# Ten products by ones into an unread bank, set among the first adaLN groups on TensorE, ahead of the first product of q

## The chip, the core and the metric

The kernel runs on one core of one Trainium2 chip. The metric is the device time of one execution in microseconds (us), the median of several runs of the same program. A core has TensorE (PE, which multiplies; PEld is its loading of weights), VectorE (DVE), ScalarE (ACT), GpSimd (POOL) and SyncE (SP, which here only issues transfers). Each works through its own instructions in order and waits on semaphores for the others. Products go to PSUM, which has eight banks of 128 partitions x 512 float32; everything else on the chip is in SBUF.

## What is computed

One step of a decoder trunk for 512 prompt positions and 8 sample positions, 1024 wide, all in float32. The part that the change touches is its beginning: the modulation of adaLN, the first RMSNorm, and the product that makes q (the other columns of `w_in`, attention, a recurrent branch and the feed-forward part follow).

```python
def rms_norm(x, g):
    xf = x.astype(jnp.float32)
    y = xf * lax.rsqrt(jnp.mean(xf * xf, axis=-1, keepdims=True) + EPS)
    return (y * g.astype(jnp.float32)).astype(x.dtype)

def ada_modulation(c, ada_w, ada_b):
    m = (jax.nn.silu(c) @ ada_w + ada_b)[:, None, :]
    return jnp.split(m, 6, axis=-1)
...
    sh1, sc1, g1, sh2, sc2, g2 = ada_modulation(c, ada_w, ada_b)
    h = rms_norm(x, norm1_g) * (1.0 + sc1) + sh1
    z = h @ w_in
```

The ten products that the change adds are no part of this: nothing reads them.

## The kernel before, in words

Everything is held transposed: features lie on the 128 partitions, the 520 positions along the row, so `x` is eight tiles `x[0]` to `x[7]` of 128 x 520. A product over all positions is made in two halves of 260 (`HALF`). To keep float32 accuracy, both factors of a large product are split into a rounded part and a rest (`whi`, `wlo` for weights, `hh`, `hl` for h), and three products of the faster type fp32r are summed: hi x hi, lo x hi, hi x lo. The small products at the beginning are made in float32 itself; for each of these the profile records two passes (two MATMUL records).

The beginning runs so:

- SP issues the loads in the order of the code: parameters (`prm`), constants (`cs`, which holds the identity and a square of ones, `ones`), the eight tiles of `x`, then eight tiles `araw` of 512 KB, the first half of adaLN's weights for shift and scale (line 473), then three loads of weights of q (`wraw`, line 510), then eight more `araw` tiles for the second half. The `araw` tiles share seven buffers, so the eighth waits until the first has been multiplied.
- ACT squares the tiles of `x`, DVE adds the squares up, and TensorE sums over partitions by multiplying with `ones` into the banks `ss1_0` and `ss1_1` (line 543: four products of 128 x 260).
- `first_mod(0, ...)` (lines 470 to 478): for each of the eight `araw` tiles (`kq` 0 to 7) four products, 32 columns wide, side by side in the array, accumulate into the bank `adaf0`. I call these four products a group. A group waits for its tile.
- `first_mod_end(0, ...)` (lines 480 to 494): ACT copies the bank (line 482), TensorE turns it by two transposes (line 485), and DVE makes the modulation from it (`mod`, line 489; `n1amp`, line 493).
- `first_h(f)` (lines 496 to 505): for each of the first four feature tiles ACT makes `hh` (line 499; the eight sample positions by a small copy, line 503), POOL the eight sample positions (lines 500, 501), DVE the exact value (line 502) and the rest `hl` (line 504). Between them ACT and DVE split the weights of q into `whi` (line 517) and `wlo` (line 518).
- `q_matmuls` (lines 522 to 528): the products of q over the first half of the features, into six banks at a time (`qp0_0`, `qp0_1` and so on). The eight groups of the second half of adaLN (`first_mod(1, ...)`, bank `adaf1`) are set among them, one after every nine products in the steady part.

TensorE takes all of this in one order, which the framework's scheduler fixes when the program is built. `tc.issue_after(m)` puts an instruction behind `m` in it. `bank(name)` takes one of the eight PSUM banks and gives it back after its last use.

Of the kernel before, what the change touches and what calls it, by code (L numbers as in the profile page):

```python
# [24 lines left out]
KT = 8  # L25
# [3 lines left out]
HALF = NT // 2  # L29
# [36 lines left out]
def kernel(ctx, tc, xT, par, gates, b_f, cst, cse, own, cache_k, cache_v, cache_lf, pt,  # L66
# [3 lines left out]
    pe, act, dve, pool, sp = nc.tensor, nc.scalar, nc.vector, nc.gpsimd, nc.sync  # L70
# [9 lines left out]
    def slot(name, cols=NT, dt=F32, parts=128):  # L80
        return heap.tile([parts, cols], dt, name=name, tag="slot")

    def bank(name, parts=128, cols=512):
        return psp.tile([parts, cols], F32, name=name, tag="bank")
# [9 lines left out]
    x = []  # L94
# [9 lines left out]
    ident = cs[:, C_ID:C_ID + 128]  # L104
    ones = cs[:, C_ONE:C_ONE + 128]
# [5 lines left out]
    silc = keep.tile([128, KT, 32], F32, name="silc")  # L111
# [47 lines left out]
    for jt in range(FF // 128):  # L159
# [5 lines left out]
        for name in BLOCKS:  # L165
            units.append((c, name, 4))
            if name in JOIN[jt]:
                g, i = JOIN[jt][name]
# [301 lines left out]
    def first_mod(fh, acc, kqs):  # L470
        for kq in kqs:
            raw = pgp.tile([128, 2, 512], F32, name="araw", tag="pg")
            sp.dma_start(raw, ada_w[kq * 128:kq * 128 + 128, :2048].rearrange("p (v c) -> p v c", v=2)
                         [:, :, 512 * fh:512 * fh + 512])
            for g in range(4):
                pe.matmul(acc[32 * g:32 * g + 32, :256], lhsT=silc[:, kq],
                          rhs=raw[:, g // 2, 256 * (g % 2):256 * (g % 2) + 256],
                          start=kq == 0, stop=kq == KT - 1, tile_position=(0, 32 * g))

    def first_mod_end(fh, acc):  # L480
        sb = slot("adas", 256)
        act.copy(sb, acc[:, :256])
        tp = bank(f"adaft{fh}")
        for b in range(2):
            pe.transpose(tp[:, b * 128:b * 128 + 128], sb[:, b * 128:b * 128 + 128], ident)
        tv = tp[:, :256].rearrange("p (b g c) -> p b g c", b=2, g=4)
        fs = slice(4 * fh, 4 * fh + 4)
        for v in (1, 0):
            dve.tensor_tensor(
                mod[:, v, fs].rearrange("p (q b) c -> p b q c", b=2), tv[:, :, 2 * v:2 * v + 2, 0:9],  # L490
                prm[:, fs, P_AB + v:P_AB + v + 1].rearrange("p (q b) c -> p b q c", b=2).to_broadcast([128, 2, 2, 9]),
                ALU.add)
        dve.scalar_tensor_tensor(amp1[:, fs], mod[:, 1, fs], 1.0, prm[:, fs, P_N1:P_N1 + 1].to_broadcast([128, 4, 9]),
                                 ALU.add, ALU.mult)
# [35 lines left out]
    def wraw():  # L530
        return wp.tile([128, KT, 256], F32, name="wraw", tag="wraw", bufs=2)

    ssq = [bank(f"ss1_{j}") for j in range(2)]
    for f in range(KT):
        t = slot("sq1")
# [5 lines left out]
        if f % 4 == 3:  # L541
            for j, (t0, t1) in enumerate(HALVES):
                pe.matmul(ssq[j][:, :HALF], lhsT=ones, rhs=sq[:, t0:t1], start=f == 3, stop=f == KT - 1)
    acc = [bank(f"adaf{fh}") for fh in range(2)]
    first_mod(0, acc[0], range(KT))
    r1 = slot("r1")
    for j, (t0, t1) in enumerate(HALVES):
# [6 lines left out]
    raw = wraw()  # L554
    q_weights(0, raw, 0, 0)
    first_mod_end(0, acc[0])
    for f in range(4):
        first_h(f)
    q_weights(0, raw, 4, 2)
    raw = wraw()  # L560
    q_weights(0, raw, 0, 4)
    for g3 in (0, 3):
        banks = [bank(f"qp{i}_{j}") for i in range(g3, g3 + 3) for j in range(2)]
        for k in range(4):
            for n in range(6):
                q_matmuls(0, g3 + n // 2, n % 2, k, banks[n])
                if g3 == 0 and n % 3 == 2:
                    first_mod(1, acc[1], (2 * k + n // 3,))
            if g3 and k == 0:
                first_mod_end(1, acc[1])  # L570
                for f in range(4, KT):
                    first_h(f)
        for n in range(6):
            t0, t1 = HALVES[n % 2]
            act.copy(qpart[g3 + n // 2][:, t0:t1], banks[n][:, :HALF])
        if g3 == 0:
            flr = slot("flr", KT * H).rearrange("p (k c) -> p k c", k=KT)
            sp.dma_start(flr, w_in[:, COL_FL:COL_FL + H].rearrange("(k p) c -> p k c", p=128))
    raw = wraw()
    q_weights(1, raw, 0, 0)  # L580
    q_weights(1, raw, 4, 2)
    raw = wraw()
# [312 lines left out]
    for i in range(KT):  # L895
        if i % 4 == 0:
            qtp.append(bank(f"qt{i}", NS))
        if i < 6:
            t = qpart[i]
            for j, (t0, t1) in enumerate(HALVES):  # L900
                b = bank(f"q{i}_{j}")
# [43 lines left out]
    g = [None] * KT  # L945
# [390 lines left out]
    g = None  # L1336
# [306 lines left out]
    for j in range(2):  # L1643
        for m in range(2 * PLAIN):
            if j == 0:
                begin(u + 3)
            b = bank(f"fi{m}_{j}")
# [89 lines left out]
```

## Time and profile before

| | |
|---|---|
| time, median of 3 runs | 1028.36 us (1027.15 to 1031.1) |
| the profiled execution | 1033.71 us, its span 1032.1 us |
| PE busy | 997.7 us (97%), 7994 records |
| DVE busy | 793.5 us (77%) |
| ACT busy | 552.5 us (54%) |
| POOL busy | 330.7 us (32%) |
| chain that ended last | PE 77%, DVE 10%, DMA 5%, ACT 4%, issue 3% |
| mean of the 16 DMA engines' traffic | 201 GB/s |

The page divides the span into 40 slices of 25.8 us; the first slice and the second hold everything that the change touches. Times inside the kernel are counted from the start of the span. A view by windows gives, for any stretch, how long each engine was busy in it, with the number of instructions in brackets, and then the clock that TensorE was granted (1.00 is full), the busy share of the DMA engines and what they moved. A timeline has one row for an instruction or a run of equal ones: start, duration, engine, line, operation, what is written and read, and, in square brackets, how long the engine had been idle and what ended that. [...] The chain of waits is the chain of work that ended last, with each piece cut at the point where the next takes over.

### The profile page before, as it was taken

To read this page: it belongs to the slowest core of one execution; us is meant where nothing else is said; L and a number is where in the kernel's file an instruction comes from. 1 tells how busy PE (TensorE), PEld (TensorE's weight loads), DVE (VectorE), ACT (ScalarE), POOL (GpSimd) and SP (SyncE) were. 2 spreads that over 40 slices of the span, in tenths; PEclk is the share of its full clock that TensorE was granted. 3 is DMA by queue.
4 is the path that set the end of the run, shared out by engine and by line. 5 is a ranking of instruction groups with operands and counts; after the bars stand their busy time and mean duration, and the time that the engine had idled before them with its cause. 6 is when DMAs were issued, how large, how long until landed. Compare 5 with 4: busy or idle time off the path is not lost.

```text
span 1032.1 us, 21298 instructions
## 1 busy us (share of the span) xinstructions
PE 997.7 (97%) x7994; PEld 922.1 (89%) x7994; DVE 793.5 (77%) x1423; ACT 552.5 (54%) x1132; POOL 330.7 (32%) x424
## 2 busy tenths in 40 slices
PE   4999999999999999999999999999999999999996
PEld 1888989999898988878888989999999999999996
DVE  5446999998999977886756544778878888888864
ACT  4433665857682266776876223555444444445453
POOL 0214511111135134554430001485433423424212
PEclk9899999999999999999999999999999999999998
DMA  9888987878898998999665784323343342333212
GB/s 330 298 270 290 306 288 210 274 230 274 260 272 297 340 322 254 295 283 275 197 240 183 251 304 139 83 62 100 86 123 88 98 124 65 99 104 102 62 63 83
DMA packets 164378, 206.98 MB, mean 201 GB/s; under 512 B 9890, under 2 KB 125106, under 8 KB 164210
## 3 DMA queue, kind: packets, MB, share of 16 engines
q1 hardware_dynamic: 147554, 152.52, 47.7%
q0 software_dynamic: 13040, 46.67, 13.8%
q10 hardware_dynamic: 3680, 6.42, 1.7%
q8 instruction: 63, 1.03, 0.4%
q14 instruction: 41, 0.34, 0.1%
HBM read 192.49 MB, written 13.09 MB: 199 GB/s over the span
## 4 chain that ended last, share of the span: by engine, by line
PE 77%; DVE 10%; DMA 5%; ACT 4%; issue 3%; POOL 1%; SPq 0%; POOLq 0%; DVEq 0%; ACTq 0%
PE fo L305 12%; PE pb L305 4%; PE gb L305 4%; PE k L305 4%; PE v L305 3%; PE ga L305 3%; PE pa L305 3%; PE wo L305 3%; PE pv L817 2%; PE gr L305 2%; PE xr L305 2%; DMA wraw<-in_w_in_dram 2%; PE qp L527 2%; PE po L1265 2%; PE q L527 1%
## 5 line engine op out<-in xcount | busy, mean ns | idle before, releaser
L246 ACT CAST whi<-wraw 128x1024 fp32r<-128x1024 f32 (+1 forms) x79 | 82.1, 1040 | 135.2 <-PE pb L305 35.3
L248 DVE TENSOR_TENSOR wlo<-wraw,whi 128x1024 fp32r<-128x1024 f32 (+1 forms) x79 | 100.1, 1268 | 31.3 <-ACT whi L246 29.2
L270 ACT CAST wb<-ws 128x512 fp32r<-128x512 f32 x72 | 44.8, 622 | 92.2 <-PE fo L305 64.4
L305 PE MATMUL fo<-ach,wb 128*128 128x260 f32 x512 | 93.2, 282 | 0.0
L682 POOL DMA_DIRECT2D pg<-in_cache_k_dram x74 | 39.4, 533 | 141.8 <-DVE S L731 76.1
L305 PEld LDWEIGHTS fo<-ach,wb 128*128 128x128 f32 x512 | 78.9, 188 | 0.0
L271 DVE TENSOR_TENSOR wb<-wraw,wb 128x512 fp32r<-128x512 f32 x86 | 74.0, 860 | 6.0 <-ACT wb L270 5.0
L261 POOL TENSOR_TENSOR ws<-wraw 128x512 f32<-128x512 f32 x18 | 26.7, 1485 | 153.7 <-DMA wraw<-in_w_fi_dram 135.1
L270 ACT CAST wb<-wraw 128x512 fp32r<-128x512 f32 x86 | 53.4, 621 | 37.1 <-ACT cp L1625 6.2
L305 PE MATMUL fo<-acl,wb 128*128 128x260 f32 x256 | 72.3, 282 | 0.0
L271 DVE TENSOR_TENSOR wb<-ws,wb 128x512 fp32r<-128x512 f32 x72 | 59.9, 832 | 15.1 <-ACT wb L270 13.3
L730 DVE TENSOR_TENSOR pg<-pg,qb 128x1024 f32<-128x1024 f32 x48 | 58.4, 1236 | 1.3 <-DMA pg<-in_cache_k_dram 1.2
L731 DVE TENSOR_REDUCE S<-pg 128x16 f32<-128x1024 f32 x48 | 57.1, 1210 | 0.1
L1222 POOL TENSOR_SCALAR p<-p,mu 128x128 f32<-128x128 f32 (+3 forms) x28 | 35.6, 1282 | 51.6 <-DVE mu L1218 39.6
L305 PEld LDWEIGHTS fo<-acl,wb 128*128 128x128 f32 x256 | 48.2, 188 | 0.0
L1216 ACT ACTIVATE p<-p,mu 128x128 f32<-128x128 f32 (+3 forms) x64 | 35.3, 553 | 13.6 <-DVE mu L1215 13.3
L305 PE MATMUL v<-hh,whi 128*128 128x260 f32 x128 | 37.9, 296 | 0.6 <-DVE pl L1236 0.3
L305 PE MATMUL pb<-oh,whi 128*128 128x260 f32 x128 | 36.9, 288 | 1.0 <-ACT oh L1323 1.0
L305 PE MATMUL k<-hh,whi 128*128 128x260 f32 x128 | 37.3, 292 | 0.0
L817 PE MATMUL pv<-pg,pw 128*32 128x512 f32 x256 | 35.1, 604 | 2.0 <-DMA pg<-in_cache_v_dram 1.8
L305 PE MATMUL ga<-hh,wlo 128*128 128x260 f32 x128 | 36.3, 284 | 0.8 <-DVE wlo L248 0.8
L305 PE MATMUL gb<-hh,whi 128*128 128x260 f32 x128 | 37.0, 289 | 0.0
(1099 smaller groups left out, 3980.6 us busy)
## 6 DMA issues: line engine op xcount, KB each, us to landing
araw<-in_ada_w_dram SPq DMA_DIRECT2D x48, 512.0 KB, 6.9
wraw<-in_w_fi_dram SPq DMA_DIRECT2D x44, 512.0 KB, 4.1
pg<-in_cache_k_dram POOLq DMA_DIRECT2D x42, 512.0 KB, 6.2
pg<-in_cache_v_dram SPq DMA_DIRECT2D x42, 512.0 KB, 5.2
wraw<-in_w_in_dram SPq DMA_DIRECT2D x34, 512.0 KB, 7.3
wraw<-in_w_in_dram SPq DMA_DIRECT2D x11, 1024.0 KB, 10.4
pg<-in_cache_v_dram POOLq DMA_DIRECT2D x22, 512.0 KB, 6.6
pg<-in_cache_k_dram POOLq DMA_DIRECT2D x32, 256.0 KB, 5.9
```

The source lines that it names most:

```text
L246: state["act"] = act.copy(hi[:, :k1 - k0], src)
L248: state["last"] = dve.tensor_tensor(lo[:, :k1 - k0], src, hi[:, :k1 - k0].bitcast(F32), ALU.subtract)
L270: state["act"] = act.copy(t[:, :4], src)
L271: state["last"] = dve.tensor_tensor(t[:, 4:], src, t[:, :4].bitcast(F32), ALU.subtract)
L305: state["mm"] = pe.matmul(out[:, :t1 - t0], lhsT=wt[k], rhs=at, start=k == 0 and m == 0, stop=k == nk - 1 and m == 2)
L527: state["mm"] = pe.matmul(b[:, :HALF], lhsT=wt, rhs=at[:, t0:t1], start=k == 0 and m == 0, stop=k == 3 and m == 2)
L682: done.append(eng.dma_start(pg, cache[bass.ds(r, 1), :, c0:c1].rearrange("a p c -> (a p) c")))
L730: dve.tensor_tensor(pg, pg, q, ALU.mult)
L731: last = dve.tensor_reduce(S[r // 2][:, c:c + H], pg.rearrange("p (h d) -> p h d", d=DH), AX.X, ALU.add)
L817: pe.matmul(pv[0][32 * gq:32 * gq + 32, :], lhsT=pw[r][:, c:c + 32], rhs=pgs[gq // 2][:, 512 * hf:512 * hf + 512], start=j == 0, stop=j == ...
L1216: act.activation(p[:, :n + 128], p[:, :n + 128], AF.Exp, bias=mu[:, 0:1], scale=-1.0, accum_out=mu[:, 1:2])
L1222: (pool.tensor_scalar(p, p, mu[:, 2:3], None, ALU.mult) if a and i + 1 < KT else act.activation(p, p, AF.Copy, scale=mu[:, 2:3]))
```

## The change

A ninth name for a bank, `idle`, is taken before the others. Behind each of the groups `kq` 2 to 7 of `first_mod(0, ...)`, TensorE multiplies the first 260 positions of `x[0]` by `ones` into it once, and behind the two transposes of `first_mod_end(0, ...)` four times: ten float32 products of 128 x 260. Nothing reads the bank. The second half of adaLN (`fh == 1`) gets none.

```diff
             for g in range(4):
-                pe.matmul(acc[32 * g:32 * g + 32, :256], lhsT=silc[:, kq],
-                          rhs=raw[:, g // 2, 256 * (g % 2):256 * (g % 2) + 256],
-                          start=kq == 0, stop=kq == KT - 1, tile_position=(0, 32 * g))
+                m = pe.matmul(acc[32 * g:32 * g + 32, :256], lhsT=silc[:, kq],
+                              rhs=raw[:, g // 2, 256 * (g % 2):256 * (g % 2) + 256],
+                              start=kq == 0, stop=kq == KT - 1, tile_position=(0, 32 * g))
+            if fh == 0:
+                keep_busy(m, 1 if kq > 1 else 0)
+
+    def keep_busy(m, n):
+        for _ in range(n):
+            with tc.issue_after(m.ins):
+                m = pe.matmul(idle[:, :HALF], lhsT=ones, rhs=x[0][:, :HALF], start=True, stop=True)
 
     def first_mod_end(fh, acc):
         sb = slot("adas", 256)
         act.copy(sb, acc[:, :256])
         tp = bank(f"adaft{fh}")
         for b in range(2):
-            pe.transpose(tp[:, b * 128:b * 128 + 128], sb[:, b * 128:b * 128 + 128], ident)
+            m = pe.transpose(tp[:, b * 128:b * 128 + 128], sb[:, b * 128:b * 128 + 128], ident)
+        if fh == 0:
+            keep_busy(m, 4)
...
+    idle = bank("idle")
     ssq = [bank(f"ss1_{j}") for j in range(2)]
```

On TensorE the place is the run of groups, the transposes and the first products of q. Before (each row is one instruction or several equal ones: line, operation, written <- read, shape, count):

```order
L543 MATMUL ss_1_115<-sq_129,cs 128x260
L476 MATMUL adaf_142<-araw,silc 32x256 x32
L485 MATMUL adaft_223<-cs,adas 128x128 x2
L527 MATMUL qp_0_276<-hh,whi 128x260
L527 MATMUL qp_0_276<-hh,wlo 128x260
```

The same place in the changed program, where lines behind 478 have other numbers (485 is the added product, 492 the transposes, 536 the products of q):

```order
L476 MATMUL adaf_143<-araw,silc 32x256 x12
L485 MATMUL idle<-x,cs 128x260
L476 MATMUL adaf_143<-araw,silc 32x256 x4
L485 MATMUL idle<-x,cs 128x260
L476 MATMUL adaf_143<-araw,silc 32x256 x4
L485 MATMUL idle<-x,cs 128x260
L476 MATMUL adaf_143<-araw,silc 32x256 x4
L485 MATMUL idle<-x,cs 128x260
L476 MATMUL adaf_143<-araw,silc 32x256 x4
L485 MATMUL idle<-x,cs 128x260
L476 MATMUL adaf_143<-araw,silc 32x256 x4
L485 MATMUL idle<-x,cs 128x260
```

Behind these rows, still in the changed program:

```order
L492 MATMUL adaft_230<-cs,adas 128x128 x2
L485 MATMUL idle<-x,cs 128x260 x4
L536 MATMUL qp_0_287<-hh,whi 128x260
L536 MATMUL qp_0_287<-hh,wlo 128x260
L536 MATMUL qp_1_288<-hh,whi 128x260
```

The 32 products of the eight groups are cut up from `kq` 2 on, one added product behind each group; four more stand between the transposes and the first product of q. Everything else stands on TensorE as it did, and the instructions of DVE, ACT and SP stand in the same order as before, with the same waits.

The second place is the third tile of q's first six banks, with the semaphores that each waits for. Before:

```order
L527 MATMUL qp_1_279<-hl,whi 128x260
L527 MATMUL qp_0_280<-hh,whi 128x260
L527 MATMUL qp_0_280<-hh,wlo 128x260 [waits DVE_49]
L527 MATMUL qp_0_280<-hl,whi 128x260
L527 MATMUL qp_1_281<-hh,whi 128x260 [waits PE_49]
```

And in the changed program:

```order
L536 MATMUL qp_1_290<-hl,whi 128x260
L536 MATMUL qp_0_291<-hh,whi 128x260 [waits PE_49]
L536 MATMUL qp_0_291<-hh,wlo 128x260 [waits DVE_49]
L536 MATMUL qp_0_291<-hl,whi 128x260
L536 MATMUL qp_1_292<-hh,whi 128x260 [waits PE_49]
```

The banks are handed out one place further on, so one product more takes a bank that TensorE itself wrote last, and waits for that older work of its own engine.

## The prediction

> **What bounds the kernel now.** I read the page first (span, busy shares, the row of granted clock), then windows over the beginning, then the chain of waits and TensorE's timeline there.
>
> ```profile
> span 1032.1 us, 21298 instructions
> PE 997.7 (97%) x7994; PEld 922.1 (89%) x7994; DVE 793.5 (77%) x1423; ACT 552.5 (54%) x1132; POOL 330.7 (32%) x424
> PEclk9899999999999999999999999999999999999998
> ```
>
> TensorE is busy for 97% of the span, so the end is set by how fast it gets through its list. A stretch at a lower granted clock costs time directly, and the second digit of the clock row (8, the slice from 25.8 to 51.6 us) says that there is one. The profiled execution took 1033.71 us, 1.6 more than its span and 5.35 more than the median of the runs, 1028.36; I work out differences in it and take them from the median.
>
> The next view cuts the time into stretches of 3.41 us: busy time of PE first, then PEld, DVE, ACT and POOL, then the granted clock, the DMA share and GB/s.
>
> ```profile
> 14.78:18.20 3.42, 3.42 (x36) 1.49 (x32) 3.39 (x3) 0.28 (x1) 0.00 (x0) 1.00 1.05 401
> 18.20:21.61 3.41, 1.73 (x24) 0.31 (x16) 3.41 (x7) 0.00 (x0) 0.00 (x0) 1.00 1.05 376
> 21.61:25.02 3.41, 1.77 (x10) 0.48 (x10) 1.88 (x6) 1.84 (x4) 0.33 (x1) 0.50 1.10 351
> 25.02:28.44 3.42, 2.93 (x12) 2.74 (x13) 3.31 (x6) 2.97 (x6) 3.19 (x6) 0.50 1.05 381
> 28.44:31.85 3.41, 3.41 (x19) 2.37 (x19) 3.41 (x6) 1.97 (x5) 1.29 (x3) 0.50 1.07 392
> 31.85:35.26 3.41, 3.41 (x34) 2.30 (x33) 0.81 (x2) 0.00 (x0) 0.00 (x0) 1.00 1.03 382
> 328.81:332.22 3.41, 2.17 (x19) 1.96 (x17) 3.41 (x7) 1.04 (x1) 0.53 (x1) 1.00 0.96 351
> 383.42:386.84 3.42, 2.52 (x16) 2.09 (x17) 3.39 (x7) 2.60 (x7) 0.40 (x2) 1.00 1.05 396
> 386.84:390.25 3.41, 3.41 (x18) 3.41 (x18) 1.47 (x10) 1.86 (x8) 0.80 (x2) 0.50 0.99 180
> 390.25:393.67 3.42, 3.42 (x25) 3.25 (x25) 0.00 (x0) 2.23 (x6) 0.89 (x2) 1.00 0.76 135
> ```
>
> The clock falls to half at 21.61, behind a stretch in which TensorE was busy for 1.73 of 3.41 us, and comes back at 31.85, behind the first stretch that was busy throughout; 2.93 of 3.42 did not bring it back. The second half-clock stretch, 386.84 to 390.25, lies on the same grid: 386.84 - 31.85 is 104 times 3.413. So the gate seems to judge stretches of 3.41 us, to fall after a sparse one and to rise after a full one. It kept full clock over 2.17 of 3.41 (at 328.81) and lost it after 2.52 of 3.42 (at 383.42, many short products), so the limit for falling is not a clean busy share.
>
> ```profile
> 12.45 2.10 PE ss L543 x4
> 15.62 6.22 DMA araw<-in_ada_w_dram
> 21.88 1.12 PE adaf L476 x8
> 23.46 0.70 PE adaft L485 x2
> 24.64 0.82 ACT hh L499
> 25.51 3.98 PE qp L527 x15
> 29.50 1.01 PE adaf L476 x8
> 30.50 2.03 PE qp L527 x10
> 32.53 0.57 PE adaf L476 x8
> ```
>
> The chain of waits runs through the eighth `araw` tile, which lands at 21.84, then the last group, the transposes, `hh` on ACT, and from 25.51 on through TensorE itself.
>
> ```profile
> 19.14 0.64 PE L476 MATMUL adaf<-araw,silc 128*32 128x256 f32 x8 [0.49 <-DMA araw<-in_ada_w_dram]
> 20.50 0.64 PE L476 MATMUL adaf<-araw,silc 128*32 128x256 f32 x8 [0.72 <-DMA araw<-in_ada_w_dram]
> 30.82 0.42 PE L527 MATMUL qp<-hh,wlo 128*128 128x260 f32 x1
> 31.04 0.42 PE L527 MATMUL qp<-hl,whi 128*128 128x260 f32 x1
> 33.50 0.28 PE L527 MATMUL qp<-hh,wlo 128*128 128x260 f32 x1
> 33.61 0.28 PE L527 MATMUL qp<-hl,whi 128*128 128x260 f32 x1
> 34.30 0.64 PE L476 MATMUL adaf<-araw,silc 128*32 128x256 f32 x8
> 36.15 0.64 PE L476 MATMUL adaf<-araw,silc 128*32 128x256 f32 x8
> 667.10 0.68 PE L404 MATMUL r<-ss,cs 128*128 128x260 f32 x2 [1.33 <-DVE ss L397]
> 667.73 0.28 PE L305 MATMUL fi<-h2h,wlo 128*128 128x260 f32 x1
> ```
>
> A product of q costs 0.22 us at half clock (30.82 to 31.04) and 0.12 at full (33.50 to 33.61). A group costs 1.12 and 0.57 in the chain. From group to group in the steady part it is 1.85 us (34.30 to 36.15), of which nine products take 1.08; so a group set among products costs 0.77 with its changeovers.
>
> **The change part by part.** It removes nothing and moves nothing; it adds ten products.
>
> *Does it hold the clock?* With the added products, TensorE has work in nearly all of 18.20 to 21.61, and in 21.61 to 25.02 it has the last group (0.57), an added product, the transposes and four more. An added product is of the same kind as those of line 404: 667.10 to 667.73 holds one of them and a product of 0.12, so 0.51 at full clock; at half it is 2.10 / 2 = 1.05 (line 543). That fills 0.57 + 5 x 0.51 = 3.1 of the 3.41 us. The stretch that lost the clock had 1.73; the fullest that failed to hold it had 2.52. I take it that the clock holds.
>
> [...]
>
> *What the held clock is worth on q.* From 25.51 to 31.85 TensorE worked 6.34 us at half clock; at full clock that is 3.17, if operands are there. They are not all:
>
> ```profile
> 26.37 0.70 DVE L504 TENSOR_TENSOR hl<-hr,hh 128x520 fp32r<-128x520 f32 x1
> 26.96 0.81 ACT L499 ACTIVATE hh<-xn,mod,n1amp 128x512 fp32r<-128x512 f32 x1
> 28.59 0.69 DVE L504 TENSOR_TENSOR hl<-hr,hh 128x520 fp32r<-128x520 f32 x1
> 30.81 0.69 DVE L504 TENSOR_TENSOR hl<-hr,hh 128x520 fp32r<-128x520 f32 x1
> ```
>
> I lay the order of the changed program over these times, with the transposes done at 24.16 as before. Four added products end at 26.2 (4 x 0.51), 0.7 later than q starts now. Six products with `hh`: 26.9. The first `hl` is there at 27.07: three products to 27.5. The second `hh` is there at 27.77: six products to 28.5. Group 0.77: 29.3. Ten products (the second `hl`, 29.28, is there): 30.5. Group, nine products, group, nine products (the third `hl`, 31.50, is in time): 34.2, and the next group starts at about 34.4. Before, it starts at 36.15. Gain **1.75 us**; the late start of 0.7 costs nothing, since `hl` and `hh` are waited for anyway. Behind that point both kernels go on at 1.85 us a round.
>
> *What the added products cost ahead of that.* Tiles land some 1.37 us apart (19.14, 20.50, 21.88). At full clock a group and an added product take 0.57 + 0.51 = 1.08 without changeovers and 0.77 + 0.51 = 1.28 with them: they keep up. At half clock they take 2.1, some 0.7 too much for each. In the profiled execution full clock comes at about 18.2 at the latest (groups at 19.14 take 0.64), so one added product runs at half clock; the groups then fall behind by about 1 us and catch up 0.1 to 0.3 a round: the last group ends between 23.0 and 23.9, where it ends at 23.0 now. The transposes, 0.70, would take about half, 0.35, and the added product ahead of them ends with ACT's copy, 0.1 later. So they end between 0.25 us earlier and 0.75 later. Where the clock rises sooner, the last group starts at 21.88 as now and ends 0.55 earlier, and the transposes 0.8. I take 0, between the ends.
>
> *The rest.* The bank: one product waits for an older one of its own engine, long finished. SP's second eight loads wait for groups that end up to 1 us later; the DMA engines are at a share of 1.05 to 1.10 then and have work queued, so nothing lands later for it. Behind 31.85 all engines follow TensorE; I count no further gain.
>
> *Sum.* The profiled execution would take 1033.71 - 1.75 = 1031.96. But where the grid lies against the kernel's start is seen in one execution only. The full stretch behind 25.51 can end anywhere from 28.9 to 32.3 (25.51 + 3.41 and + 6.83), and the profiled one, 31.85, is late. Over these positions the 6.34 us become 3.4 to 6.8, and the gain, by the same walk, 0.5 to 2. I take 1.4: 1028.36 - 1.4 = 1027.0 us.
>
> [...]
>
> **The rivals.** (A) The forecast: the clock holds and DVE's and ACT's operands take over as the bound. 1027.0.
>
> (B) Slower: the added products do not count for the gate, or come too thin, and the clock still falls at 21.61. Then those behind the last group and the transposes run at half clock, 1.05 each. The transposes wait for one (0.6 beyond ACT's copy), four hold q back by 4.2 instead of the present 1.35 us (24.16 to 25.51): q starts 3.4 us late, at 28.9. Until 31.85 it then does 2.9 us at half clock, where it did 6.34; the loss is 3.4 / 2 = 1.7 us, up to 2.5 with the groups late by 0.9. 1030.1 to 1030.9. It decides from the point where full stretches of such products fail to hold the gate. Against it: the stretch 14.78 to 18.20 was full of products only 32 columns wide, and the groups behind it ran at full speed.
>
> (C) More: the clock rises early, the groups keep up, and DVE's and ACT's chain shifts with the transposes. Then the last group gives 0.55, the transposes 0.35 and q its 3.17: 4.1 us, 1024.3. Against it: DVE works without a break from 24.5 on (3.31 of 3.42, then 3.41 of 3.41), and its `hl` set the walk above.
>
> [...]
>
> (D) Nothing: the gain is taken back by a wait. The nearest candidates are the second half's tiles:
>
> ```profile
> DMA to landing us min/median/max: 3.8/6.9/11.9
> 18.48 12.45 SPq L473 DMA_DIRECT2D araw<-in_ada_w_dram  x8
> ```
>
> The first of them is issued at 18.5 and lands at 25.4 by the median, 30.4 by the maximum; the walk wants it at 28.5, the present kernel at 29.43. At the maximum the whole gain goes. A later fall of the clock, like the one at 386.84 (3.41 us at half, 1.7 lost), can come or go as the work shifts against the grid. 1028.4.
>
> **How the numbers follow.** A 0.55, B 0.15, C 0.13, D 0.17. The time is A's, 1027.0. The range goes to C's 1024.3 and B's 1030.9; the three runs of the present kernel scatter by -1.2 and +2.7 about their median, so I widen it a little below: 1023.5 to 1031.0. A measurement of this kernel tells about 0.5% (5.1 us) from no change. No case alone passes it: faster by that needs C and a lucky scatter or a later stall that goes, slower needs B and a new fall of the clock. Faster 0.13, same 0.77, slower 0.10.
>
> **What would show it.** Right: no half clock between 21.6 and 35 us, products of q 0.12 us apart from the first, waits of TensorE on DVE `hl` and ACT `hh` in 26 to 28.5, and the fourth group of `adaf1` 1 to 2.5 us earlier against the start of the span. The step on cost is wrong if the last group of `adaf0` ends later than 24. The forecast is wrong if the clock is at 0.50 in 22 to 30 (B), if the groups of `adaf1` wait for their tiles (D), or if the gain at 36 us is not that at the end.

## The result and the profile after

| | before | after |
|---|---|---|
| time, median of 21 runs each | 1029.12 us (1027.15 to 1033.38) | 1032.52 us (1029.20 to 1039.79) |
| ratio, 95% interval | | 1.0029 [1.0017, 1.0041] |
| the profiled execution, its span | 1033.71 us, 1032.1 us | 1035.09 us, 1033.4 us |

The changed kernel is 3.4 us slower, where 1.4 us faster was forecast. That is less than the 0.5% that the prediction took for a clear difference, but the interval leaves out no change, and the time lies 1.5 us above the predicted range. The kernel before has 1029.12 us in these 21 runs, 0.8 us more than in the three from which the forecast was counted. A later set of runs of the same two kernels gave 1.0019 [1.0005, 1.0032].

The page of the changed kernel: span, busy shares, granted clock over 40 slices, and the chain that ended last.

```profile
span 1033.4 us, 21337 instructions
PE 1002.2 (97%) x8014; PEld 923.0 (89%) x8014; DVE 793.7 (77%) x1423; ACT 552.2 (53%) x1132; POOL 329.2 (32%) x424
PEclk9999999999999999999999999999999999999999
PE 83%; DVE 8%; ACT 3%; DMA 2%; issue 1%; POOL 1%; SPq 0%; POOLq 0%; DVEq 0%; ACTq 0%
```

The 8 in the second slice is gone. The windows of the changed kernel (busy time of PE, PEld, DVE, ACT, POOL, then granted clock, DMA share, GB/s; in this execution the grid happens to lie within 0.2 us of the one before):

```profile
18.20:21.61 3.41, 3.41 (x30) 1.32 (x30) 3.41 (x7) 0.00 (x0) 0.00 (x0) 1.00 1.05 381
21.61:25.02 3.41, 3.41 (x26) 1.62 (x26) 1.27 (x4) 1.10 (x3) 0.00 (x0) 1.00 1.09 349
25.02:28.44 3.42, 3.12 (x16) 2.27 (x15) 3.31 (x8) 3.03 (x7) 2.89 (x6) 1.00 1.08 382
28.44:31.85 3.41, 3.39 (x32) 2.36 (x32) 3.41 (x5) 2.61 (x6) 1.92 (x3) 1.00 1.03 381
277.61:281.02 3.41, 1.73 (x10) 1.11 (x9) 2.00 (x3) 3.37 (x6) 0.00 (x0) 1.00 0.19 44
281.02:284.44 3.42, 3.42 (x17) 1.75 (x16) 3.42 (x5) 3.42 (x10) 0.53 (x1) 0.53 0.41 123
332.22:335.63 3.41, 1.52 (x14) 1.31 (x14) 3.41 (x7) 1.04 (x1) 0.53 (x1) 1.00 0.97 383
335.63:339.05 3.42, 3.42 (x10) 0.75 (x7) 3.42 (x6) 0.00 (x0) 0.72 (x2) 0.53 0.86 329
```

The clock holds from 18 to 35 us, as forecast. It falls twice later, at 281.21 and at 335.83 us, to 0.50 for 3.41 us each time, behind a stretch in which TensorE stood for half of the window (busy for 1.73 and 1.52 of 3.41 us). Neither fall was there before.

TensorE's timeline of the changed kernel around the added products (start, duration, engine, line, operation, count, and in brackets the idle time before it and what ended it):

```profile
20.79 0.64 PE L476 MATMUL adaf<-araw,silc 128*32 128x256 f32 x8
21.36 0.71 PE L485 MATMUL idle<-x,cs 128*128 128x260 f32 x2
22.00 0.64 PE L476 MATMUL adaf<-araw,silc 128*32 128x256 f32 x8
22.57 0.71 PE L485 MATMUL idle<-x,cs 128*128 128x260 f32 x2
23.20 0.64 PE L476 MATMUL adaf<-araw,silc 128*32 128x256 f32 x8
23.77 0.71 PE L485 MATMUL idle<-x,cs 128*128 128x260 f32 x2
24.34 0.44 PE L492 MATMUL adaft<-cs,adas 128*128 128x128 f32 x2
24.61 1.92 PE L485 MATMUL idle<-x,cs 128*128 128x260 f32 x8
26.20 0.45 PE L536 MATMUL qp<-hh,whi 128*128 128x260 f32 x1
...
27.76 0.62 PE L536 MATMUL qp<-hl,whi 128*128 128x260 f32 x3 [0.22 <-DVE hl L513]
...
29.38 0.64 PE L476 MATMUL adaf<-araw,silc 128*32 128x256 f32 x8
```

A group and an added product take 1.21 us from start to start (20.79 to 22.00), so the groups no longer wait for tiles but for the products between them; the last one ends at 23.84, 0.8 later than before. The transposes end 0.6 later, q starts at 26.20 instead of 25.51, and the first `adaf1` group stands where it stood (29.38, 29.43). From there on the changed kernel is ahead. Both rows below are the transposes of the second half, before and after:

```profile
45.53 0.38 PE L485 MATMUL adaft<-cs,adas 128*128 128x128 f32 x2
```

```profile
44.41 0.38 PE L492 MATMUL adaft<-cs,adas 128*128 128x128 f32 x2
```

So 1.12 us are won at 45 us, and the profiled execution still ends with a span 1.3 us longer. The question is what happens behind 45 us.

### The profile page after: what moved, and what is told of

It reads as the page before. It is cut to its first block, busy times and chain, and to the rows that moved or that the text cites. A ratio compares the mean times of both kernels' runs of the same rounds, so it can differ in the third digit from the quotient of the medians.

```text
span 1033.4 us, 21337 instructions
## 1 busy us (share of the span) xinstructions
PE 1002.2 (97%) x8014; PEld 923.0 (89%) x8014; DVE 793.7 (77%) x1423; ACT 552.2 (53%) x1132; POOL 329.2 (32%) x424
## 4 chain that ended last, share of the span: by engine, by line
PE 83%; DVE 8%; ACT 3%; DMA 2%; issue 1%; POOL 1%; SPq 0%; POOLq 0%; DVEq 0%; ACTq 0%
PE fo L305 12%; PE pb L305 4%; PE gb L305 4%; PE k L305 4%; PE v L305 4%; PE gr L305 3%; PE ga L305 3%; PE pa L305 3%; PE wo L305 3%; PE pv L827 3%; PE xr L305 2%; PE po L1275 2%; PE qp L536 2%; PE q L536 2%; PE ada L368 2%; DVE wlo L248 1%
```

## The experiments

Every kernel has its own profile and, unless said otherwise, 10 or 12 timed runs beside the kernel before on the same chip; the ratio is to that, and "mean clock" is the mean granted clock over the kernel's runs. In the edits, "+" and "-" stand against the changed kernel; lines that only take out calls or give `keep_busy` its new width are left out. Of the names used in the expectations, "adaft1" is the pair of transposes of the second half of adaLN, near 45 us.

### Which of the products, other banks, or being early

Four edits: without the four behind the transposes; without the six among the groups; one product alone behind the first group; and the change with nine products more.

```diff
 e1_six
-        if fh == 0:
-            keep_busy(m, 4)
 e2_four
-            if fh == 0:
-                keep_busy(m, 1 if kq > 1 else 0)
 e3_bank (without the four, too)
-                keep_busy(m, 1 if kq > 1 else 0)
+                keep_busy(m, 1 if kq == 0 else 0)
 e4_back
             if g3 and k == 0:
+                for _ in range(9):
+                    pe.matmul(acc[1][:, 256:], lhsT=ones, rhs=x[0][:, :256], start=True, stop=True)
                 first_mod_end(1, acc[1])
```

> Only the six products by ones between the adaLN groups; the four behind the transposes are out. Three theories. Shift: the change gains about 1.1 us by 45 us, and what comes after (buffers and page loads met at another moment, with TensorE stalls that also drop the clock) takes back 3 to 5 us more; then this run's time follows how early adaft1 comes: with the full clock up to 30 us it leads by 0.5 to 1.5 us and the time is 1030.5 to 1033, with the clock lost at 25 us it has no lead and the time is 1029 to 1030. Banks: the unread bank moves every later bank by one place, and that alone costs the 3.4 us: 1032 to 1033. Local: in most executions the added products delay the last adaf0 group and the first product of q by more than the clock gives: the six between the groups carry the larger part of it (0.8 us of 1.4 us in the profile), 1030.5 to 1032.

> Only the four products by ones behind the transposes. Shift: the clock falls at 21.6 us as before, so the lead at adaft1 is below 0.5 us or a loss of up to 0.5 us, and the time is 1028.5 to 1030.5. Banks: 1032 to 1033, as the change. Local: the four delay the first product of q by 0.5 to 1 us at half clock, 1029.5 to 1030.5.

> The unread bank is taken, but one product by ones alone is written into it, behind the first adaLN group, where TensorE waits for the second weight tile anyway. Every later bank stands one place on, as in the change. Shift and local: as before the change, 1028.5 to 1030. Banks: as the change, 1032 to 1033.

> The change whole, and nine more products by ones (128 x 256, about 0.11 us each, 1.0 us in all) into the unread half of the second half's adaLN bank, ahead of its transposes at about 44 us: TensorE stands at 45 us where it stood before the change. Shift: what follows meets the same moments as before, so 1028.5 to 1030.5. Banks: 1032.5 to 1034. Local: 1033 to 1034, the change plus 1.0 us.

| kernel | median us | ratio [95%] | mean clock |
|---|---|---|---|
| e1_six | 1032.54 | 1.0029 [1.0009, 1.0048] | 0.9935 |
| e2_four | 1030.17 | 1.0021 [1.0003, 1.0039] | 0.9940 |
| e3_bank | 1030.49 | 1.0012 [0.9993, 1.0031] | 0.9931 |
| e4_back | 1034.66 | 1.0058 [1.0039, 1.0077] | 0.9955 |

Two of these expectations had a fault. In e3_bank not every later bank stands elsewhere: 136 of 547 do. And the nine products of e4_back were counted at 0.11 us each; its timeline shows 4.05 us for them, 0.45 each, in two records for each product (x18):

```profile
44.15 4.05 PE L581 MATMUL adaf<-x,cs 128*128 128x256 f32 x18
```

So e4_back did not put TensorE back to where it was but 2.5 us behind it, and says only that a delay of 3.9 us at 44 us costs 2 to 3 at the end. Of the other three, the six among the groups alone are as slow as the change, and the two without them lie between it and before; the intervals overlap. Local would have had e1_six with its price in the place itself, and its profile has part of it: it loses the clock at 28.6 us and is 0.5 us behind at 45. Shift, in the simple form that being early costs time, finds no support: e2_four leads by 2.2 us at 45 us in its profile and is, with e3_bank, the fastest of the four.

### Is it the products' time?

Ten products of 8 columns at the ten places; a lighter form of the change; and a second profile of each of the two kernels (one run each, no ratio).

```diff
 e5_tiny
-                m = pe.matmul(idle[:, :HALF], lhsT=ones, rhs=x[0][:, :HALF], start=True, stop=True)
+                m = pe.matmul(idle[:, :8], lhsT=ones, rhs=x[0][:, :8], start=True, stop=True)
 e7_thin
-                keep_busy(m, 1 if kq > 1 else 0)
+                keep_busy(m, 1 if kq > 3 else 0, 128)
-            keep_busy(m, 4)
+            keep_busy(m, 3)
```

> The ten added products at the same ten places, but 8 columns wide in place of 260: the same instructions, and nearly every later bank another than before the change, as in the change, but next to no TensorE time in them. Theory Path: with six of them the last adaf0 group starts at 23.0 to 23.3 us (21.6 to 22.1 us without), since an added product and a group take 1.2 us where the next tile came every 1.36 us and five groups stood ready; that and the four behind the transposes cost more than the clock gives back in most executions. Then this run has the last adaf0 group at 21.6 to 22.2 us, loses the clock there as before, and takes 1028.3 to 1030.0. Theory Banks: the time goes with the other banks, whatever the products' size: 1031 to 1033.

> The kernel before, profiled a second time. Its first profile showed the mean clock at 0.990, three windows at half clock from 21.6 us and one at 386.8 us, while its 35 timed runs had 0.9932 in the mean. Path: the first profile is not typical; this one has one or two windows at half clock between 21 and 32 us, and the adaft1 transposes 0.5 to 2.5 us ahead of 45.53 us. If it is typical after all: three windows again, transposes at 45.3 to 45.7 us.

> A lighter form of the change: one product of 128 columns (about 0.24 us) behind the groups 4 to 7 of adaf0 alone, and three of 260 behind the transposes; the banks are those of the change, one by one. Path: a group and a thin product take about 0.9 us, less than the 1.36 us between tiles, so the last adaf0 group starts at 21.6 to 22.2 us as before, the clock holds to 25 us at least, and the time is 1026.5 to 1029. Banks: 1031 to 1033.

> The changed kernel, profiled a second time. Path: no window at half clock before 35 us, the last adaf0 group at 22.9 to 23.3 us, the adaft1 transposes at 44.1 to 44.7 us again; of the 3.3 us at 277 us and the 3.1 us at 326 us, which the first profile lost to loads and to the clock, little or nothing returns, and the execution takes 1029 to 1032. Rival: they return at the same places, and the change has made these waits; 1034 to 1036.

e5_tiny: 1033.22 us, 1.0036 [1.0017, 1.0055]. This was the surprise. The clock fell at 24.3 us and stayed at half to 31.2 us, TensorE had no lead at 45 us (0.07), and the kernel is as slow as the change. So neither the products' own time nor the held clock is what makes the change slow. Path falls as the whole explanation. Banks had forecast 1031 to 1033, nearly this number.

e7_thin: 1030.90 us, 1.0019 [1.0004, 1.0034], with the banks of the change, every one. The clock held throughout (mean 0.9958), the lead at 45 us is 2.2 us, and still it is not faster than before. It loses less than Banks said, but it also leads by more than the change, so it does not settle Banks.

e6_again shows two windows at half clock (23.4 to 30.2 us) where the first profile had three, and the transposes at 44.80, 0.73 earlier. e8_twice: no half clock before 35 us, transposes at 43.91; the stalls at 277 and 326 us cost less, but another came at 114 us, with a clock fall behind it (115.8 to 119.2).

### Where is it lost?

With several profiles of each kind, the same TensorE instruction can be followed through all. The table gives its start against the first profile of before, in us, mean over the profiles; the change's row takes two profiles of the kernel as given, one more from g2_change, and two of its form with other operands (f1_cs, g1_csagain, below); before's row takes the first profile, e6_again and h1_same.

| start of TensorE's work at | 45.6 | 109 | 150 | 270 | 290 | 345 | 400 | 1023 |
|---|---|---|---|---|---|---|---|---|
| before, 3 profiles | -0.27 | -0.97 | -0.96 | -0.96 | -0.75 | -1.95 | -2.37 | -2.28 |
| the change, 5 profiles | -1.13 | -1.45 | -0.56 | -0.60 | +1.05 | +1.15 | -0.68 | -0.44 |
| difference | -0.86 | -0.48 | +0.40 | +0.36 | +1.80 | +3.10 | +1.69 | +1.84 |

The lead of 0.86 us is real. It is lost in three places: 0.9 us between 109 and 150, 1.4 between 270 and 290, 1.3 between 290 and 345; 1.4 come back up to 400 us, and then nothing changes for 600 us. At the end the profiles scatter (the change from -1.34 to +1.38, before from -4.73 to 0), so the 1.84 is rough; the runs give 2.7 us in the mean over 33 runs of the change.

All twenty profiles of this document can be followed in the same way. In the nine of kernels with four added products or fewer, TensorE loses nothing between 109 and 150 us (0.0 in the mean); in the ten of kernels with six to ten, it loses 1.1, and they end 2.7 us behind the nine. (The twentieth, e4_back, has its delay at 44 us.)

The first place is the sharpest. The chain of waits there, of the first profile of before:

```profile
74.21 15.83 DMA wraw<-in_w_in_dram
...
109.53 1.13 DVE pg L726
...
115.83 0.62 DVE xcl L339
116.49 1.46 PE gate L981 x10
```

and of the changed kernel:

```profile
101.80 6.56 DMA pg<-in_cache_k_dram
108.39 1.38 DVE pg L736
...
114.79 0.62 DVE xcl L339
115.45 1.47 PE gate L991 x10
```

Before, the chain leaves the load at 90 us and from 93 us on comes down DVE's list; every page that DVE multiplies (`pg`) is there in time. After, DVE stands and waits for a page that POOL asked for at 101.80. What is behind that page on DVE is `xc` (the input of the recurrent branch), then ACT's `xch`, its rounded part, and TensorE's `gate` waits for `xch`. That wait, in TensorE's timeline, in the order before, after, after a second time, e5_tiny:

```profile
115.41 0.51 PE L981 MATMUL gate<-xch,gws 128*128 128x260 f32 x2 [0.21 <-ACT xch L338]
```

```profile
114.36 0.51 PE L991 MATMUL gate<-xch,gws 128*128 128x260 f32 x2 [0.53 <-ACT xch L338]
```

```profile
114.66 0.50 PE L991 MATMUL gate<-xch,gws 128*128 128x260 f32 x2 [1.14 <-ACT xch L338]
```

```profile
114.88 0.51 PE L991 MATMUL gate<-xch,gws 128*128 128x260 f32 x2 [0.88 <-ACT xch L338]
```

In the eleven profiles of kernels with products behind the later `adaf0` groups (260, 128 or 8 columns wide) it is 0.47 to 1.19 us, in the nine of kernels without 0.19 to 0.25. No profile is out of order. In ten of the eleven it is this page that is late: DVE waits for it for 0.19 to 1.04 us, and in the nine not at all. In the eleventh, e4_back, DVE waits 1.67 us for ACT's `whi` of a late weight tile instead. But the eleven differ from the nine in one thing more than the place of the products: they have at least six of them, the nine at most four. No kernel here parts place from number.

The traces hold more on the late page. The landing of this page is recorded in sixteen steps; the profile counts sixteen DMA engines. The profile names the kind of one queue `instruction`, and I call a packet of it a code load. Counted from POOL's request:

| | nine profiles, up to 4 added products | ten profiles, 6 to 10 |
|---|---|---|
| fifteenth step | 5.7 to 5.8 us | 5.7 to 6.1 us |
| sixteenth step | 5.8 to 6.0 us | 6.6 to 7.4 us |
| a code load starts | from 0.7 us before the fifteenth step to 1.2 behind it | 0.9 to 2.4 us before the fifteenth step |

So one of the sixteen steps is late, by 0.8 to 1.5 us behind the fifteenth, and not the whole page. The queue of the code loads has 63 packets of 16 KB, each under way for about 1.1 us (the median is 1.10 in the first profile of before and 1.13 in that of the change):

```profile
q8 instruction: 63, 1.03, 0.4%
```

The one near this page starts when TensorE has begun 1468 to 1498 of its records (1470 before, 1482 in the change; matmuls, weight loads and a few semaphore records), in all twenty profiles, with the added ones counted in. Added products count among these records (the ten of the change are 40 of them), so it starts earlier against the rest of the work: at 109.61 us before and at 105.14 us in the change. With six or more it falls into the time in which the page is under way. That it holds up one part of the page fits all these rows, and it would go by the number of products and not by their place or size. It is my estimate and not shown: the trace does not say which engine carried a packet. Of the transfers that POOL requested, from 40 us on, with the first fifteen steps within 3 us, over all twenty profiles, the sixteenth step comes more than 0.6 us behind the fifteenth in 101 of 186 where a code load started 0.8 to 2.5 us ahead of the fifteenth, and in 456 of 1931 elsewhere. So it goes with code loads, but a code load is not the only thing that does it.

The second place is of the same kind. The chain of before runs down DVE's and ACT's lists there, too, up to TensorE at 279.87:

```profile
271.71 0.66 DVE xc L960
272.37 0.34 DVE S L785
...
272.75 0.18 ACT whi L246
...
279.33 0.49 ACT gate L982
...
279.87 1.36 PE gate L981 x9
```

The same cast of `whi` in ACT's timeline of the changed kernel, with the idle time in brackets:

```profile
273.72 1.05 ACT L246 CAST whi<-wraw 128x1024 fp32r<-128x1024 f32 x1 [7.96 <-DMA wraw<-in_w_in_dram]
```

ACT waits for a weight tile there, in all five profiles of the change (6.15 to 8.79 us) and in one of three of before (6.50). In the other two of before it stands idle for 5.9 us as well, until DVE's `S`; so what the late tile adds is 0.3 to 2.9 us. Behind it on ACT is the `xch` of another feature tile, and TensorE, which in the changed kernel reads

```profile
279.04 0.51 PE L991 MATMUL gate<-xch,gws 128*128 128x260 f32 x2 [0.78 <-ACT xch L338]
279.77 0.39 PE L991 MATMUL gate<-xcl,gws 128*128 128x260 f32 x1 [0.23 <-DVE xcl L339]
280.83 0.38 PE L991 MATMUL gate<-xch,gws 128*128 128x260 f32 x1 [0.67 <-ACT gate L992]
```

stands for half of the window and has a clock of 0.50 for the next (281.21 to 284.63), by estimate 1.7 us more (half of 3.41).

### What brings it: operand, banks, place

In the change, `x[0]` lives until the last added product. In the built program this moves heap slots of later tiles (59 names; an expectation below has 57) and drops one wait of POOL's ahead of its first page loads, and the unread bank gives most later tiles another bank. Four kernels part these:

```diff
 f1_cs (and g1_csagain): constants in place of x[0]
-                m = pe.matmul(idle[:, :HALF], lhsT=ones, rhs=x[0][:, :HALF], start=True, stop=True)
+                m = pe.matmul(idle[:, :256], lhsT=ones, rhs=cs[:, :256], start=True, stop=True)
 f2_one: only one product, 8 columns, behind the transposes
+                m = pe.matmul(idle[:, :8], lhsT=ones, rhs=cs[:, :8], start=True, stop=True)
 f3_onex: the same with x[0]
+                m = pe.matmul(idle[:, :8], lhsT=ones, rhs=x[0][:, :8], start=True, stop=True)
 f4_sixtiny
-            keep_busy(m, 4)
-                m = pe.matmul(idle[:, :HALF], lhsT=ones, rhs=x[0][:, :HALF], start=True, stop=True)
+                m = pe.matmul(idle[:, :8], lhsT=ones, rhs=cs[:, :8], start=True, stop=True)
```

> The change whole, but the ten products read the constants in place of x[0] (256 columns in place of 260). In the change, x[0] lives until the last added product, which moves the heap slots of later tiles (57 names have another address) and drops one wait that POOL made before it loaded the first pages; here slots and waits of all other engines are as before the change, while the banks are those of the change. Theory Slots (the moved slots and the dropped wait cost the time downstream): 1026.5 to 1029.5. Theory Banks: 1031.5 to 1033.5. Theory Groups (whatever stands among the adaf0 groups shifts the loads that follow): 1031.5 to 1033.5.

> One product of 8 columns of the constants behind the adaft0 transposes, and nothing else: no time to speak of, slots and POOL's waits as before the change, but the banks of nearly all later tiles are others (478 of 547, most as in the change). Banks: 1031.5 to 1033.5. Slots and Groups: 1028.5 to 1030.0.

> As the run with one product of 8 columns behind the transposes, but it reads x[0]: so the heap slots move and POOL's wait is dropped as in the change, besides the banks. Slots: 1031 to 1033.5. Banks: 1031.5 to 1033.5. Groups: 1028.5 to 1030.5.

> Six products of 8 columns of the constants behind the groups 2 to 7 of adaf0, none behind the transposes; slots and POOL's waits as before the change, banks others. Groups: 1032 to 1034, as the run with ten narrow products. Slots: 1028.5 to 1030.0. Banks: 1031.5 to 1033.5.

| kernel | median us | ratio [95%] | mean clock |
|---|---|---|---|
| f1_cs | 1031.02 | 1.0003 [0.9988, 1.0017] | 0.9962 |
| f2_one | 1029.82 | 1.0013 [0.9997, 1.0029] | 0.9928 |
| f3_onex | 1030.26 | 1.0011 [0.9992, 1.0030] | 0.9928 |
| f4_sixtiny | 1032.25 | 1.0025 [1.0006, 1.0045] | 0.9914 |

f2_one and f3_onex have the banks, f3_onex the slots as well, and both stand 1.3 us above before in the mean, where the change stands 3: nothing is seen of the slots beside the banks, and Banks can carry part of the loss at most. f4_sixtiny, with none of the slots, comes out as Groups said; part of it is local, for its clock fell at 20.1 us and stayed at half for four windows. f1_cs did not fit: by Groups it should have been as slow as the change. So change and f1_cs were put on one chip, with two lighter forms, both reading the constants:

```diff
 g3_thincs
-                keep_busy(m, 1 if kq > 1 else 0)
+                keep_busy(m, 1 if kq > 3 else 0, 128)
-            keep_busy(m, 4)
+            keep_busy(m, 3)
 g4_three: none among the groups
-            keep_busy(m, 4)
+            keep_busy(m, 3)
```

> The change itself, timed on the same chip as its form with the constants as operand. Operand (x[0] living to 24 us moves heap slots and drops a POOL wait, and that costs about 2 us downstream): 1.5 to 3 us slower than that form, at 1031.5 to 1033.5. Place (products among the adaf0 groups, whatever they read, make later loads late): within 1 us of that form.

> The change with the constants as operand (no slot moved, no wait dropped), beside the change on one chip. Operand: 1028.5 to 1031. Place: 1031 to 1033.5, as the change. In either, the mean clock is 0.995 to 0.997 against 0.993 before.

> One product of 128 columns of the constants behind the groups 4 to 7 of adaf0, three of 256 behind the transposes. Operand: 1026.5 to 1029, since the last adaf0 group is not late, the clock holds to 35 us, and no slot moves. Place: 1030 to 1032, as the same form with x[0] (1030.9); the wait for xch at 114 us is 0.5 us or more.

> Only three products of 256 columns of the constants, behind the transposes; nothing among the groups. Place: the wait for xch at 114 us is 0.19 to 0.25 us as before; the clock falls at 21 to 25 us and returns by 26 to 28 us; adaft1 leads by 1 to 2.3 us of the first profile, and the time is 1027.5 to 1029.5. Operand: the same. If other banks alone cost 1.3 us (all six forms without products of size among the groups stood 1.2 to 1.5 us above before in the mean): 1029.5 to 1031.

| kernel | median us | ratio [95%] | mean clock |
|---|---|---|---|
| g2_change | 1031.26 | 1.0019 [1.0005, 1.0032] | 0.9965 |
| g1_csagain | 1033.77 | 1.0047 [1.0028, 1.0067] | 0.9947 |
| g3_thincs | 1030.75 | 1.0011 [0.9997, 1.0025] | 0.9955 |
| g4_three | 1030.87 | 1.0013 [1.0001, 1.0026] | 0.9942 |

With the constants it is not faster but slower than the change; the operand is not the cause. But f1_cs and g1_csagain are the same program, and their intervals exclude each other: from one chip and set of runs to the next a ratio moves by more than its interval says. Differences of 0.1 to 0.2% between single kernels are not settled by these tables. g3_thincs waits 1.19 us for `xch` at 114 us, g4_three 0.24. g4_three has no product among the groups, keeps its clock all the same (below), leads by 2.55 us at 45 us, and still gives 1.0013.

### Does anything at all cost 1.4 us?

The seven kernels with a product behind each of the groups 2 to 7 (the change in both operand forms, in two sets of runs each, e1_six, e5_tiny, f4_sixtiny) stand 3.0 us above before in the mean of 91 runs, standard error 0.3 by the runs and 0.4 by the seven means, which go from 1.4 (f1_cs) to 4.9 (g1_csagain). Seven others with one, few or thin products (e2_four, e3_bank, e7_thin, f2_one, f3_onex, g3_thincs, g4_three) stand 1.2 to 1.6 us above before in the mean of their runs, 1.4 (standard error 0.3) over 84 runs together. Two kernels ask whether that is the comparison itself, or the other banks: the kernel before with one empty line more, and before with one product in the transposes' own bank.

```diff
 h2_inplace, against the kernel before
+        if fh == 0:
+            with tc.issue_after(m.ins):
+                pe.matmul(tp[:, 256:264], lhsT=ones, rhs=cs[:, :8], start=True, stop=True)
```

> The kernel before with one empty line more: the same instructions, banks, slots and waits. It is timed as every other kernel here, so it shows what the comparison itself gives for no change. If the 1.2 to 1.6 us by which all eight forms with few or thin products stand above before in the mean are real: 1028.5 to 1030, ratio within 0.0012 of 1. If they come from how a new kernel is timed beside before: 1030.3 to 1031.3 again.

> One product of 8 columns behind the adaft0 transposes, as in f2_one, but written into the unread half of the transposes' own bank: no bank, slot or order of another tile changes; the only other difference is that DVE's first mod waits for it (under 0.1 us). If the other banks cost 1.3 us: 1028.5 to 1030. If one product at this place costs it: 1030.3 to 1031.5.

h1_same: 1028.99 us, 1.0005 [0.9988, 1.0021]; its mean lies 0.3 us above before's. The comparison gives no 1.4 us for no change, though its interval reaches that far. h2_inplace: 1030.33 us, 1.0009 [0.9994, 1.0024], 1.1 us in the mean: undecided between banks and product. The two thin forms lose 0.6 us (e7_thin) and 2.5 us (g3_thincs, with a clock fall at 115.9) between 109 and 150 us; that takes g3_thincs's lead, while e7_thin's profile still ends 3.6 us ahead of the mean of before. In the profiles of the others and of h2_inplace I find no place where anything is lost, and TensorE ends 1.6 us earlier there than in the three of before, against what the runs say. This part stays open.

## Why the prediction was wrong

**Does it hold the clock?** Right: no half clock before 115 us in any of the five profiles. Over the runs the mean granted clock is 0.9958 in 33 of the change, 0.9931 in 149 of before. Rival B, the only slower one, is out.

**Gain on q.** Right in kind, less in size: 1.12 us in the profiled pair, 0.86 in the mean of the profiles, where 1.75 and 1.4 were forecast. TensorE waits for `hl` where the walk put it, but later (27.76 us against 27.07). The fourth `adaf1` group starts 1.1 us earlier:

```profile
35.03 0.64 PE L476 MATMUL adaf<-araw,silc 128*32 128x256 f32 x8
```

**Cost ahead of q.** The bounds held (last group 23.84 of 23.0 to 23.9; transposes +0.6 of -0.25 to +0.75), but I took 0 for the transposes, and it was near the upper end. A group and a product take 1.21 us where I had 1.08 to 1.28, and six of them in a row start from five groups that already stood ready, so the groups never catch up. The four products behind the transposes took 1.59 us (24.61 to 26.20), less than the 4 x 0.51 of the forecast, so q still started at 26.2 as the walk has it. But DVE and ACT start from the transposes, and with them the first `hl` came 0.7 us late. 0.6 is what the gain lacks in the profiled pair (1.75 - 1.12).

**"Behind 31.85 all engines follow TensorE; I count no further gain."** This is the step that failed, and it decides the sign. It took the page's 97% for every stage. The chain of before had shown otherwise: from 74 to 116 us, and again from 255 to 279, it runs through loads and DVE's and ACT's lists, and there a lead of TensorE is worth nothing. What I had not seen at all is that it can be worth less than nothing. The prediction says that the change "moves nothing"; but e5_tiny, whose ten products take next to no time and win no lead, is as slow as the change, so what they move does cost. In the change DVE waits 0.2 to 1.0 us for a page at 108 us and ACT waits for a weight tile at 273 us, and in some profiles the clock fell where TensorE had stood: at 281 and 335 us in the first (busy for 1.73 and 1.52 of the 3.41 us ahead of it), at 115 in the second.

**Rival D** had the right kind of mechanism, "the gain is taken back by a wait" and "a later fall of the clock", with the wrong place (the second half's `araw` tiles, which are in time) and the wrong bound: it ended at the gain, 1028.4. The wait takes the lead and 1.8 us more by the profiles, 2.7 by the runs. With that the range would have had to reach beyond 1031.0. Another 0.8 us of the distance between 1027.0 and 1032.52 is the three-run median from which the forecast was counted.

**What is shown and what is not.** Shown: in the profiles the loss lies between 109 and 345 us, in waits on loads; TensorE's longer wait at 114 us goes with six or more added products, which in all these kernels stand at least in part among the later groups (eleven profiles against nine), whatever their width, operand or effect on the clock. It does not come from the other banks alone: f2_one has those of the change, all but one, and no longer wait. In ten of the eleven it comes from one late page, of which one step in sixteen is late. The rest of the loss up to 345 us rests on five profiles against three that scatter. Not shown: that the code load makes the page late, though all rows fit it; what makes the clock fall; and whether place or number of the products decides. Six narrow products behind the transposes, and none among the groups, would part the two. The order of the instructions of DVE, ACT and SP is the same, the weight load and the page are asked for at the same distance in both (2.6 us), and the DMA engines are at a share of 0.99 to 1.10 while both are under way, in both. None of the versions tried is faster than before.

## What to carry to other kernels

Read the chain of waits stage by stage before a lead is carried to the end: where it ran through loads and a full DVE list here, a lead of 0.86 us at 45 us was a loss of 0.40 at 150, and with the DMA engines at a share of 0.99 to 1.10 it came back as a new wait, 0.19 to 1.04 us of DVE for a page. Added instructions that cost next to no time, like the ten narrow products of e5_tiny, can still go with another time of a code load: with six to ten added products it started 0.9 to 2.4 us ahead of the page's fifteenth step, and a late page goes with that. A fall of the clock that is removed in a stage where TensorE mostly waits can be worth little (two or three windows at half clock, and 0.86 us in the mean), and each later fall of the change, 3.41 us at a clock of 0.50, takes by estimate 1.7 us at once. In a kernel whose runs scatter by 2 us, take more than one profile of each, and more than one set of runs, before a single pair is read as cause and effect; and try the edit with its cost taken out (here, products of 8 columns), which tells more than any half of it.

## What the runs showed of the hardware

The granted clock changed at 21.61, 31.85, 386.83 and 390.25 us in the first profile of before, and at 281.21, 284.63, 335.83 and 339.24 us in that of the change. The stretches between, 10.24, 354.99 and 3.41 us, and 3.41, 51.20 and 3.41 us, are whole multiples of 3.413 us; these are the windows meant here. Their grid lay differently against the kernel's start: the first fall came at 21.6, 23.4 and 20.0 us in three profiles of the kernel before, with three, two and three windows at half clock. So what the change removes differs from run to run.

No busy share of TensorE, as the profile counts it, parts the windows that lose the clock from those that keep it. Windows of g4_three, on its own grid:

```profile
19.03:22.44 3.41, 1.98 (x28) 0.47 (x24) 3.41 (x7) 0.00 (x0) 0.00 (x0) 1.00 1.06 367
22.44:25.86 3.42, 2.40 (x17) 1.82 (x14) 2.67 (x7) 2.87 (x6) 1.72 (x5) 1.00 1.09 353
25.86:29.27 3.41, 3.01 (x27) 2.25 (x26) 3.37 (x6) 3.41 (x7) 2.24 (x4) 1.00 1.05 386
377.43:380.84 3.41, 2.38 (x16) 1.82 (x14) 3.37 (x7) 3.03 (x7) 1.86 (x6) 1.00 0.94 331
380.84:384.25 3.41, 3.15 (x15) 3.07 (x15) 2.08 (x11) 2.04 (x9) 0.19 (x1) 0.50 1.00 309
```

Within one execution, windows with 1.98 and 2.40 us of busy PE kept the full clock, and one with 2.38 lost it. In this execution the clock did not fall at the beginning at all (1.00 in every row from 19.03 to 29.27), with only three added products and the groups waiting for their tiles as before: what ten products were to secure was there with three. That the lie of the grid gave it is my estimate; no run here parts the grid from the three products.

Nor does a full window settle the rise, as the prediction read it. The last row above was busy for 3.15 of 3.41 us, and the clock was back behind it (from 384.25 us). In f4_sixtiny a window that was busy throughout did not bring it back:

```profile
23.49:26.90 3.41, 3.41 (x22) 1.54 (x18) 0.00 (x0) 0.88 (x3) 0.00 (x0) 0.50 1.08 363
26.90:30.32 3.42, 2.06 (x9) 1.64 (x8) 3.05 (x8) 2.77 (x6) 2.49 (x5) 0.50 1.05 384
```
